# A two-layer decoder step on one core: copies of the samples' columns on ScalarE, a higher rate of emission for the retention heads, and half an outward product emitted behind the last head

## The chip, the cores and the metric

One Trainium2 chip, one core of it. The time is the device time of one execution in microseconds (us), of the whole program. Of the kernel before, three executions were timed, and one more was taken with the hardware profiler on.

## What is computed

One inference step of two decoder layers for 512 tokens of a prompt and 32 tokens of samples (8 sequences of 4), 544 columns in all, in float32. Layer 0 mixes by sparse attention, layer 1 by retention with 4 heads of 256 key and 512 value dimensions; each is followed by a two-matrix MLP. The change touches only the retention mixer. Of the reference, its core (cut):

```python
def retention_mixer(h, state0, pos, w_in, w_out):
    z = h @ w_in
    q, k, v, g = jnp.split(z, [qk, 2 * qk, 2 * qk + vd], axis=-1)
    q = rotate(q.reshape(B, T, RET_HEADS, RET_KEY_DIM), pos)
    k = rotate(k.reshape(B, T, RET_HEADS, RET_KEY_DIM), pos) * (RET_KEY_DIM ** -0.5)
    ...
    o, S = retention_chunked(q, k, v, state0)
    o = _rms(o) * jax.nn.silu(g.astype(F32)).reshape(B, T, RET_HEADS, RET_VAL_DIM)
    return o.reshape(B, T, vd).astype(h.dtype) @ w_out, S
    ...
    # retention_chunked, for each chunk of the prompt or group of samples:
    att = jnp.einsum('bihd,bjhd->bhij', qc, kc) * decay_mask
    o = (jnp.einsum('bhij,bjhe->bihe', att, vc)
         + jnp.einsum('bihd,bhde->bihe', qc * q_decay[None, :, :, None], S))
    S = (chunk_decay[None, :, None, None] * S
         + jnp.einsum('bjhd,bjhe->bhde', kc * k_decay[None, :, :, None], vc))
```

## The kernel before

Activations lie transposed, with model dimensions on the 128 partitions and the 544 tokens along the free axis. Every product in float32 is made of three: operands are split into a high part (ScalarE copies it to the rounded type, `split_into`, L678, or L477 for weights) and a low part (DVE subtracts, L679, L478), and TensorE multiplies high by high, high by low and low by high. A dense tile is one PSUM tile "mm" of 128 x 544, of which there are two buffers. `dense8` contracts over the whole model width in 48 matmuls of 272 columns (L518), `dense4` over the 512 values of one head in 24.

For each retention head h there are: `project(h)`, four dense tiles for k and q, rotated on the way out of PSUM by DVE (L1363, L1364 for a first half; L1369, L1372 into the tiles rotb and rotc for a second) and GpSimd (L1370, L1373); `gate(h)`, four dense tiles (heads 1 and 2 load gates made earlier); `values(h)`, which takes the tiles z that `load_values` has loaded from DRAM (L1429), scales them on DVE (L1439), repeats the samples' columns four times into vrep (L1441), and transposes both on TensorE (L1445, L1449); a similar repeat, krep (L1401), stands in `project`, with the transposes L1390 and L1405; `core(h)`, the attention products (L1507, L1517), the samples' states (L1533, L1544), the product with the values (L1563), the prompt's state (L1589, copied out through the tile so, L1593 and L1594), and the norm: the sum of squares over rows (L351), a chain of twelve small DVE operations, its spread over all partitions (L361, then ScalarE L363 and DVE L364 into the tile ro), and per value tile a multiply (L1602) and a split into the operands of the outward product; and `wout(h)`, eight tiles of that product in four units, added to the residual (L672).

`during(units, gens, rate)` sets the order. It emits the dense units of the step: the gate of head h, `wout(h - 1)` and `project(h + 1)`. After each part of a dense tile it lets the side generators, `core(h)` and then `values(h + 1)`, go on by `rate`, in units of about a us of work, which is the fourth argument, 1.1 for heads 0 to 2 and 1.3 for head 3. What is emitted first has priority; a scheduler places the instructions of each engine by priority and its own timing, and from then on each engine runs its list in order. Small tiles with the tag "tz" share three buffers (a, os, so, ro, rotb, rotc, and the gates' gs and gu). z, gates and split operands share one pool.

The loop is quoted below with the functions that the change touches.

Of the kernel before, what the change touches and what calls it, by code (L numbers as in the profile page):

```python
# [30 lines left out]
AF = mybir.ActivationFunctionType  # L31
# [113 lines left out]
def decoder_step(ctx, tc, x_prompt, x_sample, cache_k, cache_v, cache_kidx, state_ret, page_table,  # L145
# [1185 lines left out]
    with ExitStack() as st:  # L1331
# [48 lines left out]
        def project(h):  # L1380
            s = ST[h] = {"v": [], "vf": None, "g": []}

            def after_k():
                kr = s["k"]
                kh, kl = s["kd"] = [rp.tile([128, 4, 256], FR, name=n) for n in ("kh", "kl")]
                for jj in range(2):
                    ps = ps_a()
                    for j in range(2):
                        for dt in range(2):
                            PE.transpose(ps[:, 256 * j + 128 * dt:256 * j + 128 * (dt + 1)],  # L1390
                                         kr[dt][:, 128 * (2 * jj + j):128 * (2 * jj + j + 1)], ident)
                    for j in range(2):
                        jb = 2 * jj + j
                        dec = cst("kdec")[:, 4 * h + jb:4 * h + jb + 1]
                        A.activation(kh[:, jb, :], ps[:, 256 * j:256 * (j + 1)], AF.Identity, scale=dec)
                        V.scalar_tensor_tensor(kl[:, jb, :], ps[:, 256 * j:256 * (j + 1)], dec, kh[:, jb, :].bitcast(FT),
                                               op0=OP.mult, op1=OP.subtract)
                    yield
                krep = rp.tile([128, 2, 4, NS], FT, name="krep", tag="km", bufs=2)
                for dt in range(2):  # L1400
                    G.tensor_copy(krep[:, dt], kr[dt][:, None, SP:].to_broadcast([128, 4, NS]))  # L1401
                yield
                ps = ps_b()
                for dt in range(2):
                    PE.transpose(ps[:, 128 * dt:128 * (dt + 1)], krep[:, dt].rearrange("p r n -> p (r n)"), ident)  # L1405
                kf = rp.tile([128, 256], FT, name="kf", tag="km", bufs=2)
                V.tensor_scalar(kf, ps[:, :256], cst("kdecs")[:, h:h + 1], None, op0=OP.mult)
                kst = s["kst"] = rp.tile([128, 256], FR, name="kst", bufs=2)
                A.activation(kst, kf, AF.Copy)
                V.tensor_tensor(kst[64:128, :], kf[64:128, :], kst[64:128, :].bitcast(FT), op=OP.subtract)  # L1410

            def after_q():
                s["strip"] = rp.tile([128, 512], FT, name="strip")
                SY.dma_start(s["strip"], c_ret[h, :, :512])
                qa = qarr[h % 2]
                for dt in range(2):
                    for bb in range(2):
                        G.tensor_tensor(qa[:, dt, bb, :, 4 * bb:4 * bb + 4],
                                        s["q"][dt][:, SP + 16 * bb:SP + 16 * bb + 16].rearrange("p (j t) -> p j t", j=4),
                                        qdec[:, h, 16 * bb:16 * bb + 16].rearrange("p (j t) -> p j t", j=4),  # L1420
                                        op=OP.mult)
                yield

            return rotated(1024 + 256 * h, "kr", s, "k", after_k) + rotated(256 * h, "qr", s, "q", after_q)
# [6 lines left out]
        def values(h):  # L1431
            s = ST[h]
            for e in range(4):
                if e == 0:
                    s["v"] += [rp.tile([128, 4, 512], FR, name=n) for n in ("vh", "vl")]
                    s["vf"] = rp.tile([128, 512], FT, name="vf", bufs=1)
                (vh, vl), vf = s["v"], s["vf"]
                z = s["z"][e]
                V.tensor_tensor(z, z, RB, op=OP.mult)  # L1439
                vr = rp.tile([128, 4, NS], FT, name="vrep")  # L1440
                G.tensor_copy(vr, z[:, None, SP:].to_broadcast([128, 4, NS]))  # L1441
                yield 0.2
                pa = ps_a()
                for j in range(4):
                    PE.transpose(pa[:, 128 * j:128 * (j + 1)], z[:, 128 * j:128 * (j + 1)], ident)  # L1445
                split_into(vh[:, :, 128 * e:128 * (e + 1)], vl[:, :, 128 * e:128 * (e + 1)],
                           pa.rearrange("p (j d) -> p j d", j=4))
                pb = ps_b()
                PE.transpose(pb[:, :128], vr.rearrange("p r n -> p (r n)"), ident)  # L1449
                A.activation(vf[:, 128 * e:128 * (e + 1)], pb[:, :128], AF.Copy)  # L1450
                if e == 3:
                    vst = s["vst"] = rp.tile([128, 512], FR, name="vst", bufs=1)
                    A.activation(vst, vf, AF.Copy)
                    for r in (1, 3):
                        V.tensor_tensor(vst[32 * r:32 * (r + 1), :], vf[32 * r:32 * (r + 1), :],
                                        vst[32 * r:32 * (r + 1), :].bitcast(FT), op=OP.subtract)
                yield 0.6
# [26 lines left out]
        def core(h):  # L1484
# [74 lines left out]
            for e in range(4):  # L1559
# [7 lines left out]
                if e == 0:  # L1567
                    pt = ps_a()
                    for i in range(4):
                        PE.transpose(pt[:, 128 * i:128 * (i + 1)], os_[:, 128 * i:128 * (i + 1)], ident)  # L1570
                    ptv = pt.rearrange("p (e j r) -> p e j r", e=4, j=4)
                    for bb in range(2):
                        V.tensor_copy(osT[:, :, 16 * bb:16 * bb + 16].rearrange("p e (j t) -> p e j t", j=4),
                                      ptv[:, :, :, 4 * bb:4 * bb + 4])
                g = s["g"][e]
                V.tensor_tensor(g[:, :SP], g[:, :SP], ps, op=OP.mult)
                V.tensor_tensor(g[:, SP:], g[:, SP:], osT[:, e, :], op=OP.mult)
# [34 lines left out]
        def during(units, gens, rate):  # L1612
            side.append([gens, rate, 0.0])
            run(units)
            settle()
            drain(gens)
            side.clear()
# [4 lines left out]
        for h in range(RH):  # L1622
            ahead = project(h + 1) if h + 1 < RH else []
            out = wout(h - 1) if h else []
            if h in GATES_KEPT:
                out[1]["before"] = lambda h=h: load_gates(h)
                out[2]["before"] = lambda h=h: kept_gates(h)
            gens = [core(h)]
            if ahead:
                ahead[1]["before"] = lambda h=h: load_values(h + 1)  # L1630
                gens.append(values(h + 1))
            during(([] if h in GATES_KEPT else gate(h)) + out + ahead, gens, (1.1, 1.1, 1.1, 1.3)[h])
        final = wout(RH - 1)
        final[0]["load"]()
    mhs = ctx.enter_context(tc.tile_pool(name="mhs", bufs=16))
# [54 lines left out]
```

## Time and profile before

| | |
|---|---|
| median of 3 executions | 1565.93 us (1563.40 to 1572.61) |
| the profiled execution, its own time | 1571.83 us |
| its span, from first to last instruction | 1569.9 us |
| TensorE busy (PE) | 1520.6 us, 97% |
| DVE, ScalarE (ACT), GpSimd (POOL) busy | 71%, 42%, 10% |
| granted TensorE clock, mean of the span | 0.987 of full speed |
| chain that ended last | TensorE 84%, DVE 9%, DMA 3%, ScalarE 2% |

The retention layer runs from about 800 to 1200 us of the span. Head 0 ends near 900 us, head 1 near 990, head 2 near 1080 and head 3 near 1155. PE is busy whenever a matmul is in flight, at whichever clock; a stretch at half clock therefore shows as busy and must be read from the column of the clock.

### The profile page before, as it was taken

The page shows a single profiled execution, that of the slowest core. Times are in us where ns is not written, and L with a number is a line of the kernel's source. Part 1 is how long each engine was busy: PE and PEld are TensorE (multiplying, and loading weights), DVE is VectorE, ACT ScalarE, POOL GpSimd, SP SyncE. Part 2 cuts the span into 40 slices and gives each one's busy share as a digit, 9 for nine tenths or more (in the row PEclk, how much of TensorE's full clock was granted, in tenths as well). Part 3 has the DMA queues.
Part 4 walks back from the last instruction along what each step waited for, and adds up shares of the span by engine and source line. Part 5 has one row for each costly group of instructions (what it writes and reads, how often), then busy time and mean ns, then how long its engine had stood idle before and what let it go on. Part 6 is the DMA issues. An engine that isn't in the chain of part 4 may idle for free.

```text
span 1569.9 us, 28355 instructions
## 1 busy us (share of the span) xinstructions
PE 1520.6 (97%) x11540; PEld 1427.3 (91%) x11540; DVE 1112.3 (71%) x2099; ACT 659.3 (42%) x1176; POOL 163.2 (10%) x165
## 2 busy tenths in 40 slices
PE   8999899999999999999999999899989999999998
PEld 6689559999999999999998988798989999999998
DVE  5599774878767766778855685867658777677663
ACT  4323663644444433555532232414236454444332
POOL 1120420100000000200012322212111000000000
PEclk9999999999999999999999989999999999999999
DMA  6433252222233223224534537282722322332212
GB/s 177 138 117 101 71 184 78 81 99 83 89 108 108 82 81 108 81 97 151 192 134 166 205 116 270 86 292 90 241 68 81 108 87 75 108 108 82 81 54 58
DMA packets 142689, 185.92 MB, mean 118 GB/s; under 512 B 12429, under 2 KB 93399, under 8 KB 142559
## 3 DMA queue, kind: packets, MB, share of 16 engines
q1 hardware_dynamic: 142490, 184.10, 35.8%
q8 instruction: 90, 1.47, 0.4%
q14 instruction: 41, 0.33, 0.1%
q10 hardware_dynamic: 68, 0.02, 0.0%
HBM read 155.03 MB, written 31.69 MB: 119 GB/s over the span
## 4 chain that ended last, share of the span: by engine, by line
PE 84%; DVE 9%; DMA 3%; ACT 2%; issue 1%; POOL 0%; SPq 0%; DVEq 0%; ACTq 0%
PE mm L518 48%; PE mm L586 22%; PE pa L586 3%; PE pb L1563 2%; PE pb L1589 1%; DVE wl L478 1%; PE pa L1533 1%; PE pb L1544 1%; PE pa L1507 1%; PE pa L1046 1%; DVE sc L813 1%; DVE m L812 1%; PE pa L1073 1%; DMA raw<-in_att_w_in_dram 1%; DVE ss L562 1%
## 5 line engine op out<-in xcount | busy, mean ns | idle before, releaser
L518 PE MATMUL mm<-xs,wh 128*128 128x272 f32 (+1 forms) x2144 | 386.9, 296 | 9.1 <-ACT xs L678 5.4
L518 PE MATMUL mm<-hs,wh 128*128 128x272 f32 x2304 | 391.8, 289 | 3.6 <-DVE x L672 2.3
L586 PE MATMUL mm<-xs,sh 128*128 128x272 f32 x1744 | 344.7, 289 | 4.8 <-ACT r L599 2.7
L518 PEld LDWEIGHTS mm<-xs,wh 128*128 128x128 f32 (+1 forms) x2144 | 318.4, 192 | 21.0 <-issue 6.6
L518 PEld LDWEIGHTS mm<-hs,wh 128*128 128x128 f32 x2304 | 327.9, 188 | 6.5 <-DVE x L672 2.9
L586 PEld LDWEIGHTS mm<-xs,sh 128*128 128x128 f32 x1744 | 276.5, 189 | 8.3 <-ACT r L602 3.5
L477 ACT ACTIVATE wh<-raw 128x1024 fp32r<-128x1024 f32 x139 | 146.6, 1056 | 317.1 <-PE mm L518 294.8
L586 PE MATMUL mm<-xs,sl 128*128 128x272 f32 x912 | 262.6, 289 | 0.0
L672 DVE TENSOR_TENSOR x<-mm,x 128x544 f32<-128x544 f32 x176 | 127.2, 723 | 165.9 <-PE mm L518 164.9
L518 PE MATMUL mm<-hs,wl 128*128 128x272 f32 x1152 | 240.3, 288 | 0.0
L518 PE MATMUL mm<-xs,wl 128*128 128x272 f32 (+1 forms) x1072 | 233.4, 294 | 0.0
L518 PEld LDWEIGHTS mm<-hs,wl 128*128 128x128 f32 x1152 | 181.8, 188 | 0.2
L478 DVE TENSOR_TENSOR wl<-raw,wh 128x1024 fp32r<-128x1024 f32 x131 | 164.1, 1254 | 22.3 <-ACT wh L477 14.5
L518 PEld LDWEIGHTS mm<-xs,wl 128*128 128x128 f32 (+1 forms) x1072 | 174.5, 191 | 4.9 <-issue 3.2
L586 PEld LDWEIGHTS mm<-xs,sl 128*128 128x128 f32 x912 | 172.3, 189 | 0.0
L678 ACT ACTIVATE sh<-ss 128x512 fp32r<-128x512 f32 x152 | 95.6, 630 | 149.8 <-PE mm L586 148.8
L679 DVE TENSOR_TENSOR sl<-ss,sh 128x512 fp32r<-128x512 f32 x152 | 104.2, 687 | 28.4 <-PE mm L586 27.4
L678 ACT ACTIVATE sh<-raw 128x512 fp32r<-128x512 f32 x114 | 72.0, 632 | 101.2 <-PE mm L586 82.6
L679 DVE TENSOR_TENSOR sl<-raw,sh 128x512 fp32r<-128x512 f32 x114 | 78.1, 685 | 13.3 <-PE mm L586 12.2
L586 PE MATMUL pa<-xs,sh 128*128 128x272 f32 x304 | 60.0, 288 | 0.0
L679 DVE TENSOR_TENSOR hs<-r,hs 128x544 fp32r<-128x544 f32 x64 | 46.1, 720 | 16.0 <-ACT hs L678 15.9
L1546 DVE SCALAR_TENSOR_TENSOR raw<-raw,pb 128x512 f32<-128x512 f32 x64 | 43.1, 683 | 17.0 <-PE pb L1544 14.5
(357 smaller groups left out, 1894.8 us busy)
## 6 DMA issues: line engine op xcount, KB each, us to landing
raw<-in_mlp_w_in_dram SPq DMA_DIRECT2D x32, 1024.0 KB
raw<-in_mlp_w_out_dram SPq DMA_DIRECT2D x32, 1024.0 KB
raw<-in_ret_w_in_dram SPq DMA_DIRECT2D x24, 1024.0 KB
raw<-in_state_ret_dram SPq DMA_DIRECT2D x32, 512.0 KB
out_dram<-raw SPq DMA_DIRECT2D x32, 512.0 KB
raw<-in_ret_w_out_dram SPq DMA_DIRECT2D x8, 1024.0 KB
raw<-in_att_w_in_dram SPq DMA_DIRECT2D x7, 1024.0 KB
kept<-r SPq DMA_DIRECT2D x24, 272.0 KB
```

Of the source, the lines that this page charges most:

```text
L477: A.activation(h, view, AF.Copy)
L478: eng.tensor_tensor(l, view, h.bitcast(FT), op=OP.subtract)
L518: PE.matmul(ps[:m, c, :HALF], w[:, k, m * t:m * (t + 1)], x[c] if isinstance(x, tuple) else x[:, HALF * c:HALF * (c + 1)], start=(k == 0 a ...
L562: V.tensor_tensor(t, a, b, op=OP.add)
L586: PE.matmul(ps, a[:, i, :], b, start=(first and i == 0 and j == 0), stop=(i == 3 and j == 2), skip_group_check=True)
L672: V.tensor_tensor(two(xT[m]), halves(ps), two(xT[m]), op=OP.add)
L678: A.activation(dst_h, src, AF.Copy)
L679: V.tensor_tensor(dst_l, src, dst_h.bitcast(FT), op=OP.subtract)
L812: V.max(out=m8, in_=sc)
L813: V.match_replace(out=sc, in_to_replace=m8, in_values=sc, imm_value=TAKEN)
L1546: V.scalar_tensor_tensor(sl, sl, gam4[h], pu, op0=OP.mult, op1=OP.add)
L1563: PE.matmul(ps[:, SP - WJ[j]:], v[:, j, 128 * e:128 * (e + 1)], a[:, AM[j]:AM[j] + WJ[j]], start=(j == 0 and v is vh and a is am[0]), stop ...
```

## The change

Four edits, all in the retention mixer. The repeats krep (8 instructions) and vrep (16) go from GpSimd to ScalarE. `core` may be asked to wait (in emission, not on the chip) until the gate's tile exists. The rates rise from 1.1, 1.1, 1.1, 1.3 to 1.4, 1.4, 1.4, 1.8. In the step of the last head, the second half of `wout(2)` (two of four units, four tiles, 96 matmuls) is emitted after the core of head 3 instead of beside it.

```diff
--- before.py
+++ after.py
@@ -1398,7 +1398,7 @@
                     yield
                 krep = rp.tile([128, 2, 4, NS], FT, name="krep", tag="km", bufs=2)
                 for dt in range(2):
-                    G.tensor_copy(krep[:, dt], kr[dt][:, None, SP:].to_broadcast([128, 4, NS]))
+                    A.activation(krep[:, dt], kr[dt][:, None, SP:].to_broadcast([128, 4, NS]), AF.Copy)
                 yield
                 ps = ps_b()
                 for dt in range(2):
@@ -1438,7 +1438,7 @@
                 z = s["z"][e]
                 V.tensor_tensor(z, z, RB, op=OP.mult)
                 vr = rp.tile([128, 4, NS], FT, name="vrep")
-                G.tensor_copy(vr, z[:, None, SP:].to_broadcast([128, 4, NS]))
+                A.activation(vr, z[:, None, SP:].to_broadcast([128, 4, NS]), AF.Copy)
                 yield 0.2
                 pa = ps_a()
                 for j in range(4):
@@ -1572,6 +1572,8 @@
                     for bb in range(2):
                         V.tensor_copy(osT[:, :, 16 * bb:16 * bb + 16].rearrange("p e (j t) -> p e j t", j=4),
                                       ptv[:, :, :, 4 * bb:4 * bb + 4])
+                while len(s["g"]) <= e:
+                    yield 1.0
                 g = s["g"][e]
                 V.tensor_tensor(g[:, :SP], g[:, :SP], ps, op=OP.mult)
                 V.tensor_tensor(g[:, SP:], g[:, SP:], osT[:, e, :], op=OP.mult)
@@ -1629,7 +1631,11 @@
             if ahead:
                 ahead[1]["before"] = lambda h=h: load_values(h + 1)
                 gens.append(values(h + 1))
-            during(([] if h in GATES_KEPT else gate(h)) + out + ahead, gens, (1.1, 1.1, 1.1, 1.3)[h])
+            if h == RH - 1:
+                out, last = out[:2], out[2:]
+            during(([] if h in GATES_KEPT else gate(h)) + out + ahead, gens, (1.4, 1.4, 1.4, 1.8)[h])
+        run(last)
+        settle()
         final = wout(RH - 1)
         final[0]["load"]()
     mhs = ctx.enter_context(tc.tile_pool(name="mhs", bufs=16))
```

What this does to the order of the instructions (in the changed kernel lines from 1575 on carry numbers higher by 2, from about 1632 on by 6):

TensorE at the end of head 0. mm_10655 and mm_10672 are the last tile of `project(1)` before and now, mm_10753 is the first tile of `wout(0)`. Before:

```order
L518 MATMUL mm_10655<-xs_7775,wh_10449 128x272 x2
L518 MATMUL mm_10655<-xs_7776,wh_10449 128x272 x2
L518 MATMUL mm_10655<-xs_7775,wl_10450 128x272 x2
L361 MATMUL pa_10545<-rw_10479,ident_103 128x136 x2
L361 MATMUL pb_10546<-rw_10479,ident_103 128x136 x2
L1449 MATMUL pb_10607<-ident_103,vrep_10598 128x128
L1390 MATMUL pa_10585<-ident_103,kr0_10368 128x128
...
L1445 MATMUL pa_10600<-ident_103,xs_10379 128x128 x4
L1449 MATMUL pb_10639<-ident_103,vrep_10630 128x128
L1449 MATMUL pb_10652<-ident_103,vrep_10643 128x128
L1405 MATMUL pb_10668<-ident_103,krep_10626 128x128 x2
```

Now:

```order
L518 MATMUL mm_10596<-xs_7775,wh_10412 128x272 x2
L518 MATMUL mm_10596<-xs_7776,wh_10412 128x272 x2
L518 MATMUL mm_10596<-xs_7775,wl_10413 128x272 x2
L361 MATMUL pa_10442<-rw_10392,ident_103 128x136 x2
L361 MATMUL pb_10443<-rw_10392,ident_103 128x136 x2
L518 MATMUL mm_10672<-xs_7529,wh_10574 128x272
L518 MATMUL mm_10672<-xs_7530,wh_10574 128x272
...
L518 MATMUL mm_10672<-xs_7775,wl_10575 128x272 x2
L518 MATMUL mm_10753<-xs_10451,wh_10745 128x272 x2
L518 MATMUL mm_10753<-xs_10452,wh_10745 128x272 x2
L518 MATMUL mm_10753<-xs_10451,wl_10746 128x272 x2
```

Before, all of `project(1)` stood ahead of L361; now its last tile of 48 matmuls, mm_10672, stands behind it, and the outward product behind that; the transposes come later, within `wout(0)`.

TensorE at the end of head 1. mm_11555 was the last tile of `project(2)`, mm_11653 and mm_11693 are the first two tiles of `wout(1)`. Before:

```order
L518 MATMUL mm_11555<-xs_7775,wh_11349 128x272 x2
L518 MATMUL mm_11555<-xs_7776,wh_11349 128x272 x2
L518 MATMUL mm_11555<-xs_7775,wl_11350 128x272 x2
L361 MATMUL pa_11445<-rw_11379,ident_103 128x136 x2
L361 MATMUL pb_11446<-rw_11379,ident_103 128x136 x2
L1449 MATMUL pb_11507<-ident_103,vrep_11498 128x128
L1390 MATMUL pa_11485<-ident_103,kr0_11268 128x128
...
L1445 MATMUL pa_11500<-ident_103,xs_11279 128x128 x4
L1449 MATMUL pb_11539<-ident_103,vrep_11530 128x128
L1449 MATMUL pb_11552<-ident_103,vrep_11543 128x128
L1405 MATMUL pb_11568<-ident_103,krep_11526 128x128 x2
L1445 MATMUL pa_11532<-ident_103,xs_11280 128x128 x4
```

Now:

```order
L1591 MATMUL pb_11305<-vl_10492,kh_10621 128x512
L1591 MATMUL pb_11305<-vh_10491,kl_10622 128x512
L361 MATMUL pa_11342<-rw_11292,ident_103 128x136 x2
L361 MATMUL pb_11343<-rw_11292,ident_103 128x136 x2
L518 MATMUL mm_11653<-xs_11351,wh_11645 128x272 x2
L518 MATMUL mm_11653<-xs_11352,wh_11645 128x272 x2
L518 MATMUL mm_11653<-xs_11351,wl_11646 128x272 x2
L518 MATMUL mm_11653<-xs_11356,wh_11645 128x272 x2
L518 MATMUL mm_11693<-xs_11351,wh_11645 128x272 x2
```

Now the twelve matmuls of L1591 (L1589 before) stand directly ahead of L361, and the outward product directly behind it; every tile of `project(2)` is placed earlier.

TensorE at the end of head 2, from L361 on. mm_12553 and mm_12671 are tiles of `gate(3)`. Before:

```order
L518 MATMUL mm_12553<-xs_7640,wh_12545 128x272 x2
L518 MATMUL mm_12553<-xs_7641,wh_12545 128x272
L361 MATMUL pa_12345<-rw_12279,ident_103 128x136 x2
L361 MATMUL pb_12346<-rw_12279,ident_103 128x136 x2
L1390 MATMUL pa_12385<-ident_103,kr0_12168 128x128
...
L1449 MATMUL pb_12407<-ident_103,vrep_12398 128x128
L518 MATMUL mm_12553<-xs_7641,wh_12545 128x272
L518 MATMUL mm_12553<-xs_7640,wl_12546 128x272 x2
```

Now (the two gate tiles of 48 matmuls each lie in the gap, with the transposes of the first z between the last of them):

```order
L1591 MATMUL pb_12205<-vh_11391,kl_11522 128x512
L361 MATMUL pa_12242<-rw_12192,ident_103 128x136 x2
L361 MATMUL pb_12243<-rw_12192,ident_103 128x136 x2
L518 MATMUL mm_12553<-xs_7529,wh_12545 128x272
...
L1449 MATMUL pb_12329<-ident_103,vrep_12320 128x128
L1445 MATMUL pa_12335<-ident_103,xs_12272 128x128 x4
...
L1449 MATMUL pb_12367<-ident_103,vrep_12358 128x128
L1405 MATMUL pb_12485<-ident_103,krep_12469 128x128 x2
L1390 MATMUL pa_12423<-ident_103,kr0_12228 128x128
...
L1517 MATMUL pb_12618<-qr0_12465,kr0_12228 32x32 x4
...
L1544 MATMUL pb_12686<-vst_12370,km_12684 128x512
```

Before, gate matmuls stood on both sides of L361 and between all of the transposes; now they begin behind L361, and the transposes of the last two z, of krep and k, and the first products of head 3 follow one another without dense work. SyncE's queue at the same place, loads of z for head 3 and stores of so for head 2. Before:

```order
L1429 DMA xs_12179<-kept12_8852 128x544
L1429 DMA xs_12180<-kept13_8910 128x544
L1429 DMA xs_12181<-kept14_8989 128x544
L1429 DMA xs_12182<-kept15_9047 128x544
...
L1594 DMA out_5_dram<-so_12271 128x512
L1594 DMA out_5_dram<-so_12341 128x512
```

Now:

```order
L1596 DMA out_5_dram<-so_12184 128x512
L1596 DMA out_5_dram<-so_12238 128x512
L1429 DMA xs_12270<-kept12_8852 128x544
L1429 DMA xs_12271<-kept13_8910 128x544
L1429 DMA xs_12272<-kept14_8989 128x544
L1429 DMA xs_12273<-kept15_9047 128x544
```

The four loads stood far ahead of the stores; now they stand right behind them, and, by the same list's waits, behind DVE's last use of the tiles that they overwrite.

At the end of head 3, `mm_13287`, the last tile of `wout(2)`, had its 24 matmuls ahead of L361 and has now 20 ahead of it and 4 behind; the other three tiles of that half stand ahead as before.

## Rows read from the trace of the kernel before

**Rows 1.** The page, its sections 1 and 4: busy time of the engines in us (share of the span) x instructions; then the chain that ended last, its share by engine.

```profile
PE 1520.6 (97%) x11540; PEld 1427.3 (91%) x11540; DVE 1112.3 (71%) x2099; ACT 659.3 (42%) x1176; POOL 163.2 (10%) x165
...
PE 84%; DVE 9%; DMA 3%; ACT 2%; issue 1%; POOL 0%; SPq 0%; DVEq 0%; ACTq 0%
```

**Rows 2.** Busy time in stretches of 50 us around the ends of head 0, head 1 and head 3: stretch, its length, busy us (x instructions) of PE, PEld, DVE, ACT, POOL, then the granted TensorE clock as a share of full speed, the share of the DMA engines, GB/s.

```profile
900.00:950.00 50.00, 45.21 (x315) 38.58 (x314) 39.32 (x65) 16.17 (x31) 13.69 (x14) 0.90 0.43 146
...
950.00:1000.00 50.00, 45.95 (x332) 42.54 (x331) 34.64 (x64) 16.94 (x34) 15.64 (x17) 0.97 0.57 192
...
1150.00:1200.00 50.00, 45.81 (x350) 44.26 (x349) 35.32 (x58) 22.41 (x36) 8.68 (x6) 0.93 0.21 69
```

**Rows 3.** Who waited for whom, TensorE's waits from 800 to 1260 us: waiting operation <- releaser: us in total, times, longest.

```profile
PE mm L518 <- ACT xs L678: 5.4, 3, 3.1
...
PE pb L1449 <- POOL vrep L1441: 4.6, 4, 2.5
...
PE mm L518 <- DVE kr L1364: 0.7, 1, 0.7
...
PE pa L1533 <- DMA raw<-in_state_ret_dram: 0.7, 1, 0.7
```

**Rows 4.** Busy time in finer stretches, columns as in group 2: behind head 0, behind head 1, around the end of head 2, behind head 3.

```profile
904.00:914.00 10.00, 8.48 (x49) 7.40 (x50) 9.65 (x20) 4.63 (x11) 4.58 (x6) 0.50 0.35 119
...
996.00:1000.00 4.00, 3.46 (x32) 3.33 (x33) 3.97 (x9) 2.72 (x6) 0.22 (x1) 0.57 0.05 8
...
1080.00:1100.00 20.00, 18.68 (x141) 14.37 (x140) 19.05 (x36) 10.79 (x22) 4.81 (x7) 1.00 0.18 65
...
1160.00:1167.00 7.00, 6.13 (x28) 6.13 (x29) 2.72 (x5) 0.87 (x2) 0.00 (x0) 0.52 0.22 87
```

**Rows 5.** Instructions in order of time behind head 0: start us, duration us, engine, line, operation, out<-in, how many in a row [idle time of the engine before <- what ended it].

```profile
900.79 2.40 POOL L1370 TENSOR_TENSOR qr<-qr,rotb 128x544 f32<-128x544 f32 x1
...
902.56 3.26 DVE L1602 TENSOR_TENSOR xs<-xs,ro 128x544 f32<-128x544 f32 x4
...
903.15 0.78 POOL L1441 COPY vrep<-xs 128x128 f32<-128x128 f32 x1
...
903.98 0.47 PE L1449 MATMUL pb<-ident,vrep 128*128 128x128 f32 x1 [2.52 <-POOL vrep L1441]
```

**Rows 6.** The same view behind head 1.

```profile
988.16 0.73 PE L361 MATMUL pa<-rw,ident 128*128 128x136 f32 x4
...
992.09 0.33 PE L1449 MATMUL pb<-ident,vrep 128*128 128x128 f32 x1 [1.20 <-POOL vrep L1441]
...
992.24 3.89 DVE L1602 TENSOR_TENSOR xs<-xs,ro 128x544 f32<-128x544 f32 x4
...
994.84 0.52 PE L518 MATMUL mm<-xs,wh 128*128 128x272 f32 x2 [1.77 <-ACT xs L678]
```

**Rows 7.** The same view at the end of head 2.

```profile
1088.69 0.27 PE L1449 MATMUL pb<-ident,vrep 128*128 128x128 f32 x1
...
1093.04 0.71 PE L1544 MATMUL pb<-vst,km 128*128 128x512 f32 x2 [1.09 <-DVE vst L1455]
```

**Rows 8.** The same view at the end of head 3.

```profile
1147.61 0.29 DVE L354 TENSOR_SCALAR rw<-pb 128x136 f32<-128x136 f32 x1
...
1150.81 0.30 DVE L337 SCALAR_TENSOR_TENSOR rw<-rw 128x136 f32<-128x136 f32 x1
...
1154.83 0.62 PE L361 MATMUL pa<-rw,ident 128*128 128x136 f32 x4
...
1155.87 1.22 DVE L478 TENSOR_TENSOR wl<-raw,wh 128x1024 fp32r<-128x1024 f32 x1
...
1157.55 2.63 DVE L1602 TENSOR_TENSOR xs<-xs,ro 128x544 f32<-128x544 f32 x4
...
1158.31 2.56 ACT L678 ACTIVATE xs<-xs 128x544 fp32r<-128x544 f32 x4 [2.19 <-DVE xs L1602]
...
1159.02 0.76 PE L518 MATMUL mm<-xs,wh 128*128 128x272 f32 x4 [3.10 <-ACT xs L678]
...
1160.09 2.62 DVE L679 TENSOR_TENSOR xs<-xs 128x544 fp32r<-128x544 f32 x4
...
1160.87 0.82 PE L518 MATMUL mm<-xs,wh 128*128 128x272 f32 x2 [1.09 <-DVE xs L679]
```

**Rows 9.** Groups of instructions by line, 800 to 1260 us: line, engine, operation, out<-in, partitions x elements, how many | busy us, mean ns of one | idle before, releaser.

```profile
L1441 POOL COPY vrep<-xs 128x128 f32<-128x128 f32 x16 | 8.2, 511 | 61.4 <-DVE xs L1439 35.9 <-PE pb L1449 25.5
...
L1401 POOL COPY krep<-kr 128x128 f32<-128x128 f32 x8 | 2.1, 291 | 0.0
...
L1450 ACT ACTIVATE vf<-pb 128x128 f32<-128x128 f32 x16 | 4.4, 273 | 7.2 <-PE pb L1449 7.2
...
L1363 DVE TENSOR_TENSOR qr<-mm,rot 128x544 f32<-128x544 f32 x4 | 2.9, 718 | 0.2 <-PE mm L518 0.2
```

**Rows 10.** The chain that ended last, in order of time: twelve matmuls of the prompt's state at the end of head 3, and a tile of an outward product; start us, us, what, instructions.

```profile
1147.53 2.80 PE pb L1589 x12
...
1236.90 3.00 PE mm L518 x24
```

**Rows 11.** Instructions in order of time: SyncE issues loads of rows kept in DRAM, and DVE's first use of one (columns as in group 5).

```profile
911.77 3.52 SPq L1462 DMA_DIRECT2D xs<-kept  x3
...
914.54 0.72 DVE L1466 TENSOR_TENSOR xs<-xs,RB 128x544 f32<-128x544 f32 x1 [0.79 <-DMA xs<-kept]
```

## The prediction

> **What bounds the kernel.** I read the page first. TensorE is busy 97% of the span and 84% of the chain that ended last is its own [rows 1], so a change in emission order can only win or lose what TensorE idles, and what it runs at half clock. Next I took the retention layer (800 to 1260 us) in stretches. The four ends of heads stand out. Around the end of head 0 TensorE is busy 45.21 of 50 us at a mean granted clock of 0.90; around the end of head 1 45.95 at 0.97; around the end of head 3 45.81 at 0.93 [rows 2]. The finer stretches give the clock: 0.50 for the 10 us behind head 0, 0.57 for 4 us behind head 1, 0.52 for 7 us behind head 3, so half speed (1.2 instead of 2.4 GHz) each time, but 1.00 at the end of head 2, where TensorE idles 1.3 of 20 us [rows 4]. Price of each end, idle plus lost clock: 0 to 1: 4.8 - 0.7 (a late state load, which the change does not touch [rows 3]) + 5.0 = 9.1 us; 1 to 2: 4.0 + 1.7 = 5.7; 2 to 3: 1.3; end of head 3: 4.2 + 3.4 = 7.6. Together some 24 us: the most that can be won here. The list of waits says what for: the first split operand of an outward product (ScalarE xs, 5.4 us in 3 waits) and vrep on GpSimd (4.6 in 4) [rows 3].
>
> Behind head 0 the reader sees GpSimd take a rotation of 2.40 us ahead of a copy vrep, TensorE standing 2.52 us for that copy, and the clock going down right then [rows 5]. Behind head 3 there is no GpSimd work: TensorE has nothing between the transposes at L361 and the first product, 3.10 us, and 1.09 more for the low half [rows 8].
>
> **The copies (first part).** 24 copies leave GpSimd (8.2 + 2.1 us) and cost ScalarE about 24 x 0.273 = 6.6 us by the like-sized copy at L1450 [rows 9]. ScalarE is 42% busy [rows 1], so they cost nothing themselves, except that at a head's end up to three stand in ScalarE's queue ahead of the split xs: 0 to 0.8 us, taken as 0.3 at each of three ends, so 0.9. The vrep waits go. The rotations stay on GpSimd. On GpSimd a copy takes 0.29 us [rows 9], but 0.78 when a DVE multiply runs (903.15); four DVE multiplies take 3.26 us while GpSimd works [rows 5], and 3.89 behind head 1 [rows 6], against 2.63 behind head 3, where it is idle: they end at 1160.2 as the low halves start [rows 8]. The Trainium skill, "SBUF — State Buffer", section Who interferes with whom, says that a DVE operation with two SBUF inputs and a GpSimd operation that reads SBUF hold one port pair in turn; these rows agree, and by that rule alone the departure of the copies gives DVE back what such a copy lasts too long, 0.78 - 0.29 = 0.5 us, at each of the two ends, so that the sum would be 1 us lower.
>
> **Higher rates: end of head 0 (gain).** With more of the side work emitted per dense step, heads end earlier relative to the dense work. At 0 to 1 the order shows a whole tile of project(1), 48 matmuls, behind L361, where before only transposes and vrep stood. Runs of 24 take 3.00 us [rows 10], so 6.0 us cover the chain from L361 to the first split operand, which takes 4.19 us behind head 3 [rows 8]. Left are about 1 to 3 us: the new tile needs a PSUM buffer that DVE frees only after the chain of the norm. I expect no fall of the clock. Gain 9.1 - 2.1 = 7 us (6 to 8).
>
> **Higher rates: inside heads 1 and 2 (loss).** The second tile of k keeps its PSUM buffer until the norm's chain is done, so q's second tile must wait for the two evacuations of q's first, 2 x 0.72 us [rows 9]. The nearest wait of this kind lasts 0.7 [rows 3]. Twice 1.4 = 2.8 us; 0 if other work fills it, 6.8 if q's weights come 2 us late behind the state's DMAs as well.
>
> **Higher rates: end of head 1 (loss).** All of project(2) is used up before the last product of the core. Between L351 and L361 only 12 matmuls (2.8 us) [rows 10] stand, while DVE's chain takes from 1147.61 to 1150.81 for ten steps, so 0.32 each, 4 us for twelve, and some 0.6 ahead of it: 1.7 us of idleness, and 0.3 at L351. Behind L361 the outward product follows directly: 4.19 us in head 3, of which 1.1 are L361 itself and up to 1.2 a weight's split (1155.87) [rows 8]: 2.5. Then the low halves: 1.09 in head 3, here with two rotations of 0.72 on DVE in between: 2.1. Idle 6.6, and clock between 1.7 and 5.0, taken as 3.4 [rows 4]: 10.0 against 5.7 now, so a loss of 4.3 (2 to 7). For the small end speaks that vrep's 1.20 us and the late split's 1.77 [rows 6] go with GpSimd's copies.
>
> **Higher rates: end of head 2 (the largest loss).** Before, dense tiles of gate(3) stand on both sides of L361 and between the transposes of z. Now L351 and L361 stand bare as above (2.0 us), and the first gate tile waits for the second rotation, whose buffer has to leave by DMA first (1.25). The four loads of z (L1429) are moved in SyncE's queue past both DMAs of so (L1594 before, L1596 now), and wait for g tiles that the splits of head 2 free. A like load took from 911.77 to 914.54, 2.8 us, until DVE could multiply [rows 11]. First tiles free some 5 us after L361, then 2.8 us of load and 0.72 of multiply: z0 comes at about 8, z3 at 11 to 12, z0 hidden by 12 us of gate tiles. But the rest of the chain (z2 and z3 transposed, vrep, k transposed, vst, then L1544) comes when those tiles are used up. In the kernel before it takes 1093.04 - 1088.69 = 4.35 us from the last vrep to L1544, of which only 1.09 are idle [rows 7]; now one more round of split and transpose (1.3) stands ahead of it with no dense work to fill. I take 4 us of idleness, 0.5 in the head's first products, and 0 to 1.4 until DVE has emptied the next gate tile, 0.7. Idle 2.0 + 1.25 + 4 + 0.5 + 0.7 = 8.5 against 1.3; clock 0 to 3.4, taken as 0.8, since transposes stand between the stops: a loss of 8 (5 to 11).
>
> **Half of wout(2) behind the last head (nothing).** The order shows that it is not left behind: the scheduler pulls it forward, and of its 96 matmuls 4 follow L361. They hide 0.5 of the 7.6 us: -0.5 (-1 to +0.5). The added guard on g never has to wait; it issues nothing.
>
> **The sum.** 0.9 - 7 + 2.8 + 4.3 + 8 - 0.5 = +8.5 us on the profiled execution (1571.83, of which 1569.9 are the span). That execution lies 5.9 above the median, 1565.93; added to the median: 1574.4. The ends of the terms together give -2 to +21, so 1564 to 1587.
>
> **Rivals.** What a measurement of this kernel can tell from no change is about 0.5%, 7.8 us: below 1558.1 is faster, above 1573.8 slower.
>
> *GpSimd was the whole of it (faster).* If the bare chains at the ends of heads 1 and 2 run at the pace of head 3 once GpSimd copies nothing, then from L361 to the first split operand it is 4.19 us instead of 6.7 (988.16 to 994.84) [rows 6, 8]: 2.5 won behind head 1, clock kept; and if the z's come before the 12 us of gate tiles are used up, head 2's end costs what it does now. With 7 at head 0 that is 9.5, so 1556. It decides at L1544 of head 3: under 1.5 us idle there, and it holds. Against it: no dense work in the order at either place.
>
> *Gain and loss cancel (no change).* All losses at their lower ends (0 + 0 + 2 + 5 - 0.5) against 7: 1565.4. The case in which the half of wout(2) would cover head 3's end after all (7 us less than my sum, 1567.4) lies here too; the order speaks against it.
>
> *Both new gaps also lose the clock (much slower).* Behind head 0 a stop of 2.52 us, with little work about it, was followed by 10 us at half speed [rows 4, 5]. If both new ends go that way, 5.0 instead of 3.4 and 0.8: 1.6 + 4.2 = +5.8 on my sum, and late weights +4: 1584. The Trainium skill, "TensorE: Matmul & The Clock Gate", section HAM oscillation, says that an engine which idles between bursts falls back to the lower clock each time and pays for it again; by it this rival would be the likeliest. The end of head 2, with 1.3 us idle and clock 1.00 [rows 4], is the case against taking it for short stops.
>
> **How the numbers follow.** My forecast 0.35, much slower 0.12: slower 0.47, though the forecast stands just above its bound. No change 0.31. Faster 0.22. Predicted time 1574.4. The range takes in the faster rival's 1556 and, nearly, the upper end of the sum: 1556 to 1586.
>
> **What would show it.** In the changed profile: no wait for vrep on GpSimd; no half-clock stretch behind head 0, and under 3 us idle there; a stop of TensorE ahead of L361 and of the first outward product behind head 1; in head 3 L1439 waiting for the DMA of z, and L1544 for vst; behind head 3 still 4 us or so of idleness. I am wrong if TensorE stays busy from L361 to L1544 behind head 2, or if head 0's end keeps its gap.

## The result, and where the time went

The changed kernel takes 1586.83 us (median of 4 executions, 1585.84 to 1593.22), the kernel before 1566.08 in the same comparison: ratio 1.0135, 95% interval 1.0094 to 1.0176. Slower, as forecast, but by more than twice what was forecast, and 0.8 us above the range. In all later comparisons, with 17 to 29 executions each, the kernel before had a median of 1568.4 to 1568.6, so part of the distance to the forecast is its basis: 1566 was the median of a few executions.

The profiled execution took 1587.69 us, 15.9 more than the one of before. The page: TensorE's busy time grew by 4.8 us, from 1520.6 to 1525.4, and its span by 16.0, from 1569.9 to 1585.9; so 11.2 us of the difference are idleness.

```profile
PE 1525.4 (96%) x11540; PEld 1426.6 (90%) x11540; DVE 1116.9 (70%) x2099; ACT 664.6 (42%) x1200; POOL 154.6 (10%) x141
```

Busy time in stretches of the changed kernel, columns as in [rows 2]:

```profile
900.00:950.00 50.00, 47.42 (x358) 40.62 (x357) 40.47 (x65) 17.59 (x36) 12.52 (x11) 1.00 0.41 135
...
950.00:1000.00 50.00, 42.05 (x269) 37.44 (x264) 31.54 (x57) 12.19 (x22) 12.12 (x10) 0.92 0.62 211
...
1050.00:1100.00 50.00, 44.59 (x313) 40.60 (x312) 34.66 (x59) 16.44 (x35) 13.98 (x11) 1.00 0.56 181
...
1100.00:1150.00 50.00, 45.68 (x321) 38.01 (x320) 33.02 (x63) 13.31 (x25) 5.51 (x5) 0.97 0.55 190
...
1150.00:1200.00 50.00, 45.64 (x317) 43.53 (x316) 29.32 (x47) 18.32 (x30) 11.78 (x8) 0.93 0.29 95
```

The kernel before around the end of head 2, with the same columns:

```profile
1050.00:1100.00 50.00, 48.69 (x352) 42.44 (x351) 34.73 (x64) 18.97 (x38) 14.20 (x16) 1.00 0.36 123
1100.00:1150.00 50.00, 50.00 (x359) 45.78 (x358) 28.78 (x52) 11.23 (x18) 8.47 (x7) 1.00 0.64 216
```

Against these and [rows 2]: the end of head 0 (900 to 950) now loses nothing to the clock. The half-clock stretch of 10 us has moved to the end of head 1 (950 to 1000, 0.92), the end of head 2 (1050 to 1150) has become more idle (90.27 of 100 us busy instead of 98.69), and the end of head 3 has stayed as it was. The mean granted clock of the span is 0.987 in both, and from 900 to 1200 us TensorE ran 20.5 us at half clock in both, so in all the clock cost as much as before; the loss is stops. Who was waited for, 800 to 1290 us, columns as in [rows 3]:

```profile
PE mm L518 <- ACT xs L678: 6.3, 2, 4.2
PE mm L518 <- DVE xs L679: 4.6, 3, 2.2
PE pb L1544 <- DVE km L1541: 3.3, 1, 3.3
PE mm L518 <- DVE qr L1364: 2.5, 3, 1.0
PE mm L518 <- DVE x L672: 2.3, 2, 1.3
PE pa L361 <- DVE rw L338: 2.0, 2, 1.0
PE mm L518 <- DVE rotc L1372: 1.4, 1, 1.4
```

vrep has gone from 4.6 to 0.9 us. What has come: km (k for one sample, masked by DVE) in front of L1544, the rotations (qr, rotc) that hold a PSUM buffer, and L361. Where they stand, in order of time (start, duration, instruction [idle before <- what ended it]):

```profile
895.41 0.73 PE L518 MATMUL mm<-xs,wh 128*128 128x272 f32 x4 [0.61 <-DVE qr L1364]
...
902.60 0.52 PE L518 MATMUL mm<-xs,wh 128*128 128x272 f32 x2 [0.67 <-DVE xs L679]
...
987.88 0.73 PE L361 MATMUL pa<-rw,ident 128*128 128x136 f32 x4 [0.96 <-DVE rw L338]
...
993.26 0.82 PE L518 MATMUL mm<-xs,wh 128*128 128x272 f32 x2 [4.18 <-ACT xs L678]
...
995.74 0.82 PE L518 MATMUL mm<-xs,wh 128*128 128x272 f32 x2 [1.66 <-DVE xs L679]
...
1080.47 0.73 PE L361 MATMUL pa<-rw,ident 128*128 128x136 f32 x4 [1.04 <-DVE rw L338]
...
1083.05 0.77 PE L518 MATMUL mm<-xs,wh 128*128 128x272 f32 x4 [1.39 <-DVE rotc L1372]
...
1099.23 0.33 PE L1449 MATMUL pb<-ident,vrep 128*128 128x128 f32 x1 [0.94 <-ACT vrep L1441]
...
1104.34 1.19 PE L1544 MATMUL pb<-vst,km 128*128 128x512 f32 x2 [3.27 <-DVE km L1541]
...
1173.62 0.77 PE L518 MATMUL mm<-xs,wh 128*128 128x272 f32 x4 [2.14 <-ACT xs L678]
...
1176.61 0.82 PE L518 MATMUL mm<-xs,wh 128*128 128x272 f32 x2 [2.22 <-DVE xs L679]
```

The first two rows are the end of head 0: 0.61 and 0.67 us where [rows 5] show 2.52. The next three are the end of head 1: L361 late by 0.96, then nothing for 4.18 until the first split operand, then 1.66 until a low half. The next four are the end of head 2, ending with the 3.27 us in front of L1544, and the last two the end of head 3 (2.14 and 2.22 against 3.10 and 1.09 in [rows 8]).

Why head 1's and head 2's ends are bare is read from the loads of z for the next head. First before, then now, SyncE's issues and DVE's first multiply:

```profile
861.89 1.89 SPq L1429 DMA_DIRECT2D xs<-kept  x4
...
870.02 0.72 DVE L1439 TENSOR_TENSOR xs<-xs,RB 128x544 f32<-128x544 f32 x1 [0.68 <-DMA xs<-kept]
...
892.73 6.50 SPq L1594 DMA_DIRECT2D out_dram<-so  x2
```

```profile
887.80 6.34 SPq L1596 DMA_DIRECT2D out_dram<-so  x2
...
902.57 4.23 SPq L1429 DMA_DIRECT2D xs<-kept  x4
...
908.68 2.71 DVE L1439 TENSOR_TENSOR xs<-xs,RB 128x544 f32<-128x544 f32 x4
```

Before, the loads go out 31 us ahead of the stores of so and the multiplies begin at 870, 24 us ahead of L351 (893.9). Now they go out 15 us behind the stores, 14 us behind L351 (888.8), and z is multiplied from 908.68 on. So the next head's values, and with them its core, start later: its first attention product (L1507) comes 41 us after L351 instead of 24.5, while the dense work goes on as before. First before, then now:

```profile
918.41 1.88 PE L1507 MATMUL pa<-qr,kr 128*128 128x512 f32 x4
```

```profile
929.77 3.17 PE L1507 MATMUL pa<-qr,kr 128*128 128x512 f32 x8
```

Heads 1 and 2 then reach L361 with no dense work left ahead of it. The distance from one head's L351 to the next grew from 89.0, 85.8 and 77.5 us to 94.6, 92.6 and 84.7.

To compare stages that no longer lie at the same times, I sum for TensorE, over all matmuls of a stage, the time from a matmul's start to the next one's start, less the usual interval of its kind at full clock (the 20th percentile over the traces compared). That counts idleness, stops too short for the list of waits, and lost clock together. An "end" runs from 4 us ahead of a head's L351 to 32 us behind it. The length below is from the first product that waits for k of head 0 (810.15 in the kernel before) to the first of the next layer's MLP that waits for L599 (1257.55); it doesn't depend on how the execution started. Single entries do depend on what is taken as a kind: with line and shape, or these and the next product, they come out by up to 2 us other, but the stages that lose stay the same.

| us lost | before | changed | rates alone | changed, z loads earlier | late z loads alone | tied tiles (all) |
|---|---|---|---|---|---|---|
| to the end of head 0 | 6.5 | 7.7 | 8.2 | 7.7 | 6.5 | 6.5 |
| end of head 0 | 10.9 | 6.0 | 6.3 | 10.8 | 10.9 | 7.4 |
| in head 1 | 4.6 | 7.6 | 7.5 | 4.6 | 5.0 | 4.1 |
| end of head 1 | 9.1 | 12.8 | 13.1 | 11.2 | 12.6 | 6.3 |
| in head 2 | 3.5 | 6.9 | 6.7 | 4.0 | 4.6 | 3.1 |
| end of head 2 | 6.2 | 13.0 | 13.5 | 7.0 | 11.5 | 5.1 |
| in head 3 | 2.0 | 6.0 | 6.8 | 3.7 | 4.6 | 1.9 |
| end of head 3 | 8.2 | 8.5 | 7.8 | 7.7 | 6.9 | 5.0 |
| length of the stretch | 447.4 | 463.8 | 464.5 | 451.8 | 458.5 | 437.5 |

### The profile page after: what moved, and what is told of

It reads as the page before. It is cut to its first block, busy times and chain, and to the rows that moved or that the text cites. A ratio compares the mean times of both kernels' runs of the same rounds, so it can differ in the third digit from the quotient of the medians.

```text
span 1585.9 us, 28389 instructions
## 1 busy us (share of the span) xinstructions
PE 1525.4 (96%) x11540; PEld 1426.6 (90%) x11540; DVE 1116.9 (70%) x2099; ACT 664.6 (42%) x1200; POOL 154.6 (10%) x141
## 4 chain that ended last, share of the span: by engine, by line
PE 84%; DVE 10%; ACT 2%; DMA 2%; issue 1%; POOL 0%; SPq 0%; DVEq 0%; ACTq 0%; POOLq 0%
PE mm L518 47%; PE mm L586 21%; PE pa L586 3%; PE pb L1563 2%; PE pa L1507 1%; PE pb L1591 1%; DVE sc L813 1%; PE pa L1533 1%; DVE xs L1604 1%; PE pa L1046 1%; PE pb L1544 1%; DVE m L812 1%; DVE wl L478 1%; PE pa L1073 1%; DVE xs L679 1%
## 5 line engine op out<-in xcount | busy, mean ns | idle before, releaser
L679 DVE TENSOR_TENSOR sl<-ss,sh 128x512 fp32r<-128x512 f32 x152 | 104.3, 688 | 28.7 <-PE mm L586 27.7
L679 DVE TENSOR_TENSOR sl<-raw,sh 128x512 fp32r<-128x512 f32 x114 | 78.3, 687 | 13.2 <-PE mm L586 12.2
L679 DVE TENSOR_TENSOR hs<-r,hs 128x544 fp32r<-128x544 f32 x64 | 46.3, 723 | 16.0 <-ACT hs L678 15.9
```

What stands on the lines that cost most here:

```text
L679: V.tensor_tensor(dst_l, src, dst_h.bitcast(FT), op=OP.subtract)
```

## The experiments

The theory after the result: the loss comes from where the z loads land in SyncE's queue. `load_values` takes its tiles when the second unit of `project(h + 1)` is emitted. At the higher rate the core's last splits have been emitted by then; they have taken the tiles that the outward product frees, and the loads get the gates' tiles, which are free only when the head is over. (The addresses in the two programs agree: before, z for heads 1 to 3 lies where split operands lay that TensorE had read; now it lies on the four gates of the running head, last read by the split in L679.) Its rivals: the rate itself (more side work per dense step than DVE and ScalarE can follow), and ScalarE's queue (copies ahead of the split operands).

**The copies alone.** The two lines of the first edit on the kernel before:

```diff
-                    G.tensor_copy(krep[:, dt], ...)
+                    A.activation(krep[:, dt], ..., AF.Copy)
...
-                G.tensor_copy(vr, ...)
+                A.activation(vr, ..., AF.Copy)
```

> The kernel before with the first edit alone: krep and vrep copied by ScalarE, rates and everything else as before. Theory 'late loads' (the loss comes from the z loads that the higher rate pushes behind the splits): the copies are harmless and take the four vrep waits (4.6 us) away, 1560 to 1564 us. Theory 'ScalarE' (copies in ScalarE's queue ahead of the split operands delay each head's end): 1570 to 1575 us.

Measured: 1567.55 us against 1568.57, ratio 0.9991 (0.9974 to 1.0009). No effect, so neither theory's numbers held: 4.6 us of waits went, and others took their place. The end of head 0, in order of time:

```profile
897.68 0.33 PE L1449 MATMUL pb<-ident,vrep 128*128 128x128 f32 x1 [0.94 <-ACT vrep L1441]
...
900.32 1.28 PE L518 MATMUL mm<-xs,wh 128*128 128x272 f32 x4 [1.41 <-ACT xs L678]
...
903.72 1.11 PE L1445 MATMUL pa<-ident,xs 128*128 128x128 f32 x4 [1.75 <-DVE vl L679]
```

vrep is waited for still (0.94, now on ScalarE), then a split operand (1.41), then a low half (1.75), and the clock falls as before. Here the waits that were removed were inherited by the next links of the chain.

**The rates alone.** On the kernel before:

```diff
-            during(([] if h in GATES_KEPT else gate(h)) + out + ahead, gens, (1.1, 1.1, 1.1, 1.3)[h])
+            during(([] if h in GATES_KEPT else gate(h)) + out + ahead, gens, (1.4, 1.4, 1.4, 1.8)[h])
```

> The kernel before with the rates 1.4, 1.4, 1.4, 1.8 alone, copies on GpSimd. Late loads: the whole loss is here, 1583 to 1592 us, with TensorE stopping at the same places as in the changed kernel. Theory 'ScalarE': under 1575 us.

Measured: 1586.72 us against 1568.57, 1.0103 (1.0078 to 1.0129). This lies in the range of the first theory. The whole loss is here, stage by stage (table), so ScalarE's queue is not its cause.

**The half of wout(2) alone.**

```diff
+            if h == RH - 1:
+                out, last = out[:2], out[2:]
...
+        run(last)
+        settle()
```

> The fourth edit alone on the kernel before. In its order no matmul of wout(2) follows L361 of head 3, as before: if the edit does nothing, 1566 to 1571 us and the same stop of 3.1 and 1.1 us. If emission order alone moves it: 1561 to 1564 us.

Measured: 1568.12 against 1568.45, 1.0000 (0.9983 to 1.0017). The edit does nothing: TensorE stands behind L361 as before.

```profile
1151.84 0.76 PE L518 MATMUL mm<-xs,wh 128*128 128x272 f32 x4 [3.10 <-ACT xs L678]
...
1153.69 0.82 PE L518 MATMUL mm<-xs,wh 128*128 128x272 f32 x2 [1.09 <-DVE xs L679]
```

In the changed kernel it does even less: without this edit the order of every engine is the same row for row.

**The z loads one unit earlier.** The changed kernel with

```diff
-                ahead[1]["before"] = lambda h=h: load_values(h + 1)
+                ahead[0]["before"] = lambda h=h: load_values(h + 1)
```

> The changed kernel with one difference: the loads of z for the next head are emitted one unit of project earlier, so that they take tiles that the outward product has freed and not gates of the running head. Late loads: the bare stops behind heads 1 and 2 go, since values and core of the next head start some 10 us earlier, 1556 to 1568 us. Theory 'rate' (more side work per dense step outruns DVE and ScalarE whatever the loads do): at least 1578 us.

Measured: 1573.56 against 1568.57, 1.0027 (1.0010 to 1.0044): 5.6 us above the upper end that I gave this theory (1568), 4.4 below the other's 1578. The loads lie ahead of the stores again, and the wait in front of head 3's L1544 falls from 3.27 to 1.44:

```profile
856.09 1.88 SPq L1429 DMA_DIRECT2D xs<-kept  x4
...
884.19 6.32 SPq L1596 DMA_DIRECT2D out_dram<-so  x2
...
1089.99 0.70 PE L1544 MATMUL pb<-vst,km 128*128 128x512 f32 x2 [1.44 <-DVE km L1541]
```

Of the 16.4 us that the stretch had grown, 12.0 are back. With them the gain at the end of head 0 has gone too: nearly all of the last tile of project(1) now runs ahead of L361 (895.11). That it does so because z is there early is argued, not shown.

**Late loads without higher rates.** The converse: the kernel before, with `load_values` called behind the core's last split and not from `project`.

```diff
-            yield 1.0
+            (h + 1 < RH) and load_values(h + 1); yield 1.0
...
-                ahead[1]["before"] = lambda h=h: load_values(h + 1)
+                pass
```

> The kernel before with its own rates and GpSimd copies; the only difference is that the z loads of the next head are emitted behind the splits of the running head, as the high rates bring about in the changed kernel. Late loads: the loss comes without any higher rate, 10 to 18 us, so 1578 to 1587 us, with a wait of L1544 in head 3 and late cores in heads 1 to 3. Theory 'rate': no loss, 1566 to 1571 us.

Measured: 1580.66 against 1568.45, 1.0070 (1.0044 to 1.0096), within the range of the first theory, and 11.1 us on the stretch. The loads alone bring stops like those of the changed kernel, though head 3's stands at the transposes of z and not at L1544:

```profile
903.45 2.23 SPq L1429 DMA_DIRECT2D xs<-kept  x4
...
991.64 1.27 PE L518 MATMUL mm<-xs,wh 128*128 128x272 f32 x4 [3.15 <-ACT xs L678]
...
1091.21 1.94 PE L1445 MATMUL pa<-ident,xs 128*128 128x128 f32 x8 [3.03 <-DVE xs L1439]
```

Rate without late loads costs 4.4 us of the stretch, late loads without rate 11.1, both together 16.4. The two losses are not made of the same things. With late loads alone TensorE ran 34.1 us at half clock from 880 to 1200 us, where before and in the changed kernel it was 20.5, so up to 6.8 of the 11.1 us are clock. Nor do the late loads by themselves hold up the next core by 16 us. Its first product, in the run with the earlier loads and then in this one:

```profile
918.54 1.88 PE L1507 MATMUL pa<-qr,kr 128*128 128x512 f32 x4
```

```profile
919.53 1.88 PE L1507 MATMUL pa<-qr,kr 128*128 128x512 f32 x4
```

L351 of head 0 stands at 885.3 and 887.4 in these runs, so the core starts 33.2 us behind it with the rate alone and 32.1 with the late loads alone, against 24.5 before and 40.9 with both: each adds about 8 us.

**Rate 1.4 for head 0 alone**, with the copies on ScalarE: `(1.4, 1.1, 1.1, 1.3)[h]`.

> Copies on ScalarE and the rate 1.4 for head 0 alone, the others as before. Late loads: only head 1's z come late, so head 0's end gains 5 to 7 us, head 1 and its end lose 6 to 8, head 2's end is as before: 1562 to 1570 us. Theory 'rate': heads 1 and 2 run at 1.1, so nothing is lost there and 0's end gains: 1556 to 1560 us.

Measured: 1571.05 against 1568.57, 1.0011 (0.9993 to 1.0030), not told apart from no change, and 1.1 us above the upper end of the first theory. Head 0's end wins 4.9 us (6.0 lost instead of 10.9) and the middle of head 1 loses 4.2 (8.8 instead of 4.6): the gain is given back within one head. The longest stop in that middle, and then L361 of head 1, which is late:

```profile
943.06 0.50 PE L1544 MATMUL pb<-vst,km 128*128 128x512 f32 x1 [1.17 <-DVE raw L1546]
...
988.16 1.28 PE L361 MATMUL pa<-rw,ident 128*128 128x136 f32 x4 [2.09 <-DVE rw L338]
```

**Rates 1.25, 1.25, 1.25, 1.5**, with the copies on ScalarE, at which the z loads keep their place (for head 1 they go out at 862.24, 28 us ahead of the stores of so).

> The changed kernel with rates 1.25, 1.25, 1.25, 1.5 and without the half left for last. In its order the z loads stand ahead of the stores of so, as before, though the rates are higher. Late loads: it is not the rate but the loads' place, so this stays within 6 us of the kernel before, 1565 to 1574 us. Theory 'rate': half way between, 1576 to 1580 us.

Measured: 1574.75 against 1568.43, 1.0038 (1.0023 to 1.0052), just above the 1574 of the first theory and below the 1576 of the other. So the rate has a price of its own, 4 to 6 us, as in the run with earlier loads. It does not grow with the rate between these two runs (on the stretch 6.3 us at 1.25, 4.4 at 1.4), and what it consists of was not taken apart.

**Dense tiles tied behind L361.** What the change was near to: dense work behind L361, with z loads and rates as before. `spread_rows` keeps its last matmul, and the last tiles are emitted behind the core, each matmul ordered behind that one (with the copies on ScalarE; the other edits are of bookkeeping):

```diff
+            spread_mm[:] = [PE.matmul(pp[j // 2][:, QT * (j % 2):QT * (j % 2 + 1)], ...)]
...
+                    with behind(after_mm):
                         PE.matmul(ps[:m, c, :HALF], w[:, k, m * t:m * (t + 1)],
...
+            last = []
+            if h in (0, 1):
+                ahead[2]["before"] = ahead[3]["load"]
+                ahead, last = ahead[:3], ahead[3:]
+            if h == RH - 1:
+                out[2]["before"] = out[3]["load"]
+                out, last = out[:3], out[3:]
             during(...)
+            after_mm[:] = spread_mm
+            run(last)
+            settle()
+            after_mm.clear()
```

The last unit of wout(2) alone:

> Copies on ScalarE, rates as before; the last unit of wout(2), two tiles of 24 matmuls (6 us), is tied behind the matmuls L361 of head 3, which the changed kernel's emission did not achieve. If the stop at head 3's end (4.2 us and 2.6 to 3.4 of clock) is there because nothing stands behind L361: TensorE runs on through it, 2 to 3 us stay ahead of L361, 1561 to 1564 us against 1567.6 of the copies alone. If the dense work is missed ahead of L361 just as much: no gain, 1566 to 1570 us.

Measured: 1565.07 against 1568.43, 0.9979 (0.9966 to 0.9992), between the two ranges. The stop behind L361 is gone; 2.22 us ahead of L361 have come in its place. The two tiles of project alone:

> Only the two project tiles tied behind L361, with the copies on ScalarE, head 3 as before. Half of what the run with all three gains: 1557 to 1563 us; if the next head's q comes late by it: 1567 us or more.

Measured: 1560.76 against 1568.43, 0.9960 (0.9945 to 0.9975), as expected. Both:

> As the run with the last unit of wout(2) tied behind L361, and the last tile of project(1) and of project(2), 48 matmuls each, tied behind L361 of heads 0 and 1 in the same way, with rates and z loads as in the kernel before. Dense work behind L361 without late loads: the ends of heads 0, 1 and 3 fall from some 10, 10 and 8 us to 3 to 5 each, 1552 to 1560 us. If the work is missed ahead of L361 or in the next head instead: 1565 us or more.

Measured: 1558.56 against 1568.43, 0.9943 (0.9926 to 0.9961), as expected. The kernel before is beaten by 9.9 us, on the stretch too, and the changed one by more. The end of head 0 in order of time, then stretches of 50 us with columns as in [rows 2]:

```profile
890.90 0.96 PE L361 MATMUL pa<-rw,ident 128*128 128x136 f32 x4 [2.08 <-DVE rw L338]
...
892.57 1.06 PE L1390 MATMUL pa<-ident,kr 128*128 128x128 f32 x4
...
893.49 1.25 PE L518 MATMUL mm<-xs,wh 128*128 128x272 f32 x4
```

```profile
850.00:900.00 50.00, 47.32 (x328) 42.82 (x327) 32.96 (x61) 15.87 (x33) 10.00 (x6) 0.97 0.60 203
...
950.00:1000.00 50.00, 46.94 (x343) 42.65 (x342) 35.34 (x60) 17.95 (x37) 13.79 (x11) 1.00 0.45 154
...
1100.00:1150.00 50.00, 47.77 (x332) 43.46 (x331) 30.71 (x57) 13.71 (x22) 5.45 (x4) 0.97 0.53 178
```

Behind L361, where the changed kernel and the one before stood, there is now the tile that was tied; what is left is 2.08 us ahead of L361, the chain of twelve small DVE operations. The three stretches hold the ends of heads 0, 1 and 3 and are busy for 47.32, 46.94 and 47.77 of 50 us, at a clock of 0.97, 1.00 and 0.97; [rows 2] had 45.21 to 45.95 at 0.90 to 0.97. Much of the gain is clock: from 880 to 1200 us TensorE ran 6.8 us at half clock instead of 20.5, which is worth up to 6.8 of the 9.9 us.

## Why the prediction was right in kind and wrong in size

- **What bounds the kernel, and the copies.** Right that only stops and clock count. The copies, taken at +0.9 us, cost 0.3 on the stretch.
- **End of head 0.** Predicted a gain of 7 (6 to 8), with no fall of the clock: 4.9, and no fall. The mechanism held; the size lies under its lower bound, for 6.0 us are still lost there where 2.1 were taken.
- **End of head 1.** Predicted +4.3, with 1.7, 0.3, 2.5 and 2.1 us of stops: +3.7 in the table; L351 0.23, L361 0.96, first split operand 4.18, low half 1.66, and the 10 us at half clock. That the two figures lie so close is partly luck. The stops come to 7.0 us where 6.6 were summed, and the clock to 5.1 where 3.4 were taken, counted in the same way, so this end was priced 2.1 us too low; but the table also has 9.1 us lost there before, where the prediction counted 5.7.
- **End of head 2.** Predicted +8: +6.8. The wait for z hid as worked out, L1544 waited 3.27 where 4 were taken, and the first gate tile waited 1.39 for rotc where 1.25 were taken. But L1544 waited for km and not, as forecast, for vst: in DVE's list km stands behind vst's subtraction and the low halves of k:

```profile
1100.77 1.38 DVE L1455 TENSOR_TENSOR vst<-vf,vst 32x512 fp32r<-32x512 f32 x2
...
1103.85 0.61 DVE L1541 TENSOR_SCALAR km<-kst,cr 128x256 fp32r<-128x256 f32 x2
```

- **Half of wout(2).** Predicted that it would do next to nothing (-0.5): it does nothing.
- **Inside the heads: the step that failed.** It was sized at 2.8 us, as two hand-overs of q's tile, with 6.8 as its bound. Those hand-overs came (waits for qr in the list above), 0.86 and 1.02. But the stages to the end of head 0 and in heads 1, 2 and 3 together lost 11.6 us more than before (28.2 against 16.6); with the other kinds named above the table it is 8.3 and 9.2, above the bound as well. I saw that the z loads had moved behind the stores and followed that to the end of head 2 only. The late loads also hold up the start of the next core, by some 8 us, the higher rate by as much again, and both together by 16. The runs with only one of the two causes lose 3.4 (rate) and 4.1 (late loads) in these stages, together they lose 11.6. Only about 2 us of that are the two hand-overs that the term was made of; most of the rest is stops too short for the list of waits. What they wait for, and how the two causes add up to more than their sum, was not taken apart and stays open.
- **The basis.** Adding the sum to the median of three executions put the forecast some 2.5 us low by the later median of 1568.5. The sum, +8.5, against +15.9 between the profiled executions, is the larger part of the miss: 7.4 of 12.4 us. The upper ends of its own terms reached 1587 and so took in the result, but by luck: the terms at the ends of heads 1 and 2 were allowed more than they came to, and the one inside the heads less.
- **The rivals.** "GpSimd was the whole of it" fell: with the copies alone nothing changes, and at L1544 of head 3, where it was to hold with under 1.5 us idle, there were 3.27. "Both new gaps also lose the clock" was right about the end of head 1 (0.92 in its 50 us) and partly for head 2 (0.97), but in sum the lost clock stayed the same, so what it adds is not where the miss lies. The Trainium skill's rule in "TensorE: Matmul & The Clock Gate", section HAM oscillation, agrees with both ends: head 1's stop of 4.18 us and head 2's of 3.27 each brought a stretch at half clock. But the fall behind head 0 went away, so that the price moved from one head's end to another's.

## What to carry to other kernels

When work is emitted in another order and tiles come from a shared pool, look first at which tile each early load is given and who frees it: a load that gets a tile of the running stage can't be early, and everything behind it starts late. Follow a late load to the start of the next stage, not only to its first waiter. To cover a chain at a stage's end, tie the covering work behind it; emission order, or a rate, leaves it to the scheduler, which pulls ready work forward.

## What was not expected of the hardware

Executions of the same first layer differ at their start. The profiled ones, one of each kernel, show a granted clock of 0.95, 0.98 or 1.00 in the first 100 us (5, 3 and 4 of 12 traces), though the edits don't touch that layer. The kernel before, then the one with the copies alone, columns as in [rows 2] but of TensorE only:

```profile
0.00:100.00 100.00, 89.33 (x575) 0.95 0.50 151
```

```profile
0.00:100.00 100.00, 88.13 (x608) 1.00 0.53 159
```

In the second the first layer's work is ahead by 4 to 5 us: the same product stands at 810.15 in the one and at 805.39 in the other. Over all twelve traces it stands at 809.8 to 810.8 where the clock was 0.95, and at 803.1 to 806.1 where it was 0.98 or 1.00. That is about half of the spread of a kernel's times, and whole profiled executions of the one group should not be set against one of the other; from the retention layer on, the two agree (447.4 and 447.7 us).
